# A hybrid decoder layer on one core: the queues' order from a plan in the source instead of from the framework

## The chip, the cores and the metric

One core of a Trainium2 chip runs the whole program. The metric is the device time of one execution in microseconds (us). PE is the matrix engine (PEld its weight loads), DVE the vector engine, ACT the scalar engine, POOL the general one, SP the queue that issues most of the DMAs. Each engine takes its instructions in the order in which they were issued to it, and waits on semaphores for the others.

## The reference

One layer over 1024 tokens of 1024 channels, in float32: a token mixer with two groups, then an MLP.

```python
h = rms_norm(x, g_mix_norm)
q, kc, vc, ks_, vs_, kw_, vw_, gl, hc, cg, bg = split(h @ w_in)
k_cmp, v_cmp = compress(kc), compress(vc)       # small two-layer MLPs over blocks of 32 tokens
# 8 heads of 64 in 2 groups; per head three causal softmax branches with a distance penalty:
#   compressed blocks, selected blocks of 64 tokens (16 of 16: all), a window of 512 tokens
attn_out = sum over branches of sigmoid(gl) * softmax(...) @ v
conv_out = bg * short_conv(cg * hc)             # 3 taps per channel
x = x + concat(rms_norm(attn_out), rms_norm(conv_out)) * g_out @ w_o
x = x + square(relu(rms_norm(x, g_ffn_norm) @ w_up)) @ w_down      # 1024 -> 4096 -> 1024
```

## The kernel before

Every large product is computed in float32 by three products of the PE's faster 32-bit type: each operand is split into a high part (an ACT copy, `copy_act`, line 69) and a low part (a subtraction on DVE or POOL, `tt`, line 66), and `mm3` (lines 76 to 78) issues high x high, high x low and low x high into one PSUM bank. The whole order of the source is one pass over these stages:

- Norm of x, transposed into `hTh`/`hTl` (eight blocks of 128 tokens, `tb`); the input product by tokens for keys, values, gates and queries (`zp`), with the steps of the compression (`compress_steps`, a generator) taken in between; then the convolution's channels (`zc`).
- The convolution's half of the output product (`wc`), and the keys' transposes.
- Attention, by token block in the order `ORDER` and by head group g. `scores` writes score products into two PSUM banks (`s_`, lines 509 and 510), DVE adds the penalty, copies them to `pt` and finds the extreme in one instruction (line 517, `nm`), ACT takes the exponential (line 523). `weigh` transposes the probabilities (line 618, `tp`), splits them into `ph` and `pl`, multiplies by the values (lines 630 and 631, `ot`), transposes back (`ops`, line 638) and adds to `osb`. Its steps are kept in the list `filler` and are spread by hand over the scores of the next group. `queries` loads `qx` from DRAM and transposes it (`tpq`, line 544). `finish` does the output product of one block (`wa`) and the norm's factor for the MLP.
- The MLP runs as Strassen-like products with seven instead of eight block products. `turn` (line 769) transposes differences of token blocks into the operands B11, B21, T2, T1, T3, B22, T4, through two PSUM banks (tag "up"). `up_raw` loads 1 MB of w_up for one pair of 128-wide hidden tiles and scales it by the norm's weight in eight ACT instructions. `product` splits one weight block and issues 12 matmuls; `pair` does the rest of a pair: sums into the tiles `d`, the square of the ReLU, and the stores of seven combinations to DRAM (`u_d`). The A11 and A12 products of the pairs 0 to 2 stand in the source ahead of the last transposes, as filling.
- The down product takes two pairs at a time through the same seven steps: it loads `ur`, splits it into `uu` (ten of each half, eight `ur`), splits the weights into `we` (six), and adds each PSUM result to `y`.

Buffers come from pools, which are opened and closed at the stage borders; a tile's slot is handed on in a ring. The source runs under the framework's tile scheduler with `TCARGS = dict(schedule_with_timeline_sim=True)`: the framework simulates the engines with costs of its own, and orders the queues from the order of the source. Two places override it with `tc.issue_after`: the weights of the output product are issued behind the second load of queries, and the scaling of w_up for pair q behind an ACT copy of pair q-2 (`marks`).

Of the kernel before, what the change touches and what calls it, by code (L numbers as in the profile page):

```python
# [1 line left out]

# [21 lines left out]
G = 2  # L24
# [10 lines left out]
QUADS = ((0, 1, 2, 3), (4, 5, 6, 7))  # L35
HEADS = (0, 2, 1, 3)
EPS = 1e-6
TCARGS = dict(schedule_with_timeline_sim=True)
BIG = 1e35
C_KV = AW  # L40
# [2 lines left out]
GELU_C = 0.7978845608028654  # L43


@with_exitstack
def trunk_layer(ctx, tc, x, g_mix_norm, w_in, g_q, g_k, pe_cmp, w_cmp1, b_cmp1, w_cmp2, b_cmp2,
                conv_w, g_out, w_o, g_ffn_norm, w_up, w_down, out):
    nc = tc.nc
    x2d = x.rearrange("b t d -> (b t) d")  # L50
    out2d = out.rearrange("b t d -> (b t) d")
    w_in, g_q, g_k, pe_cmp = w_in[0], g_q[0], g_k[0], pe_cmp[0]
# [3 lines left out]
    def pool(stack, name, bufs=1, side=None, space=None):  # L56
        kw = {}
        if side is not None:
            kw["side"] = side
        if space is not None:  # L60
            kw["space"] = space
        return stack.enter_context(tc.tile_pool(name=name, bufs=bufs, reuse_waits="tile", **kw))


    def tt(eng, o, a, b, op):
# [2 lines left out]
    def copy_act(o, i, scale=1.0):  # L68
        nc.scalar.activation(o, i, AF.Copy, scale=scale)  # L69
# [14 lines left out]
    cst = pool(ctx, "cst")  # L84
    st = pool(ctx, "st", bufs=3)
    ident = cst.tile([P, P], F32, name="ident")
    make_identity(nc, ident)
# [133 lines left out]
    with ExitStack() as b1:  # L221
# [129 lines left out]
        for tb, ps in (a for tbs in QUADS for a in z_tokens(pieces, tbs, 512, steps, 1)):  # L351
# [12 lines left out]
                                               dup(gq_bc), op0=ALU.mult, op1=ALU.mult)  # L364
            nc.scalar.dma_start(q_d[tb * P:(tb + 1) * P], qn.rearrange("p h a d -> p (h a d)"))


    with ExitStack() as b2:
        mcp = pool(b2, "mcp", side="right")
# [57 lines left out]
        KH = [kp.tile([P, KW], F32R, name=f"KH{g}") for g in range(G)]  # L427
        KL = kp.tile([P, KW], F32R, name="KL")
        half = [slice(g * HD, (g + 1) * HD) for g in range(G)]
        VC.append(kp.tile([P, G, P], F32R, name="vco"))  # L430
        nc.gpsimd.memset(VC[1][:64].bitcast(F32), 0.0)
        copy_act(VC[1][64:], VC[0][:64].bitcast(F32))

        def split_keys(g, c0, n, ps):
            copy_act(KH[g][:, c0:c0 + n], ps)
# [159 lines left out]
    with ExitStack() as c_:  # L595
# [3 lines left out]
        pq = pool(c2, "pq", bufs=2, side="right")  # L599
        pts.append(pool(c2, "pt1", side="right"))  # L600
        wo_pc = []

        def load_wo():
            for c in range(4):
                wo_pc.append(w_piece(wov[:, c:c + 1], [P, 1, D], gcol=G_OUT + c,
                                     alloc=lambda sh: (e1.tile(sh, F32, name="w_raw", tag="x"), wo_p.tile(sh, F32R, name="w_hi"), wo_p.tile(sh, F32R, name="w_lo"))))
# [189 lines left out]
        marks = {}  # L796

        def up_raw(q):
            raw = (ex.tile([P, KD, 2 * P], F32, name="wu", tag="x") if q % 3 == 0 else
                   vp.tile([P, KD, 2 * P], F32, name="wu", tag=("vs", "vw")[q % 3 - 1]))  # L800
            nc.sync.dma_start(raw, wuv[:, :, q * 2 * P:(q + 1) * 2 * P])
            with tc.issue_after(marks[q - 2]) if q > 2 else ExitStack():
                for k in range(KD):
                    copy_act(raw[:, k], raw[:, k], scale=cols[:, G_FFN + k:G_FFN + k + 1])
            return {f"A{i + 1}{j + 1}": raw[:, 4 * j:4 * j + 4, i * P:(i + 1) * P] for i in range(2) for j in range(2)}

        def w_unit():
# [86 lines left out]
    def pair(q, A, ps, done):  # L894
        D0, D1, D2, D3 = [None] * 4

        def square(a):
            nc.vector.scalar_tensor_tensor(a, a, 0.0, a, op0=ALU.max, op1=ALU.mult)  # L898
# [43 lines left out]
        nc.scalar.activation(D1[:, 0], D1[:, 0], AF.Square)  # L942
# [52 lines left out]
    for c in range(NPAIR // CHUNK):  # L995
        qs = range(c * CHUNK, (c + 1) * CHUNK)
        Bs = [down_raw(q) for q in qs]
        if c == 0:
            for tb in [th * 4 + j for th in TH for j in range(4)]:
                yacc[tb] = ey.tile([P, D], F32, name=f"y{tb}")  # L1000
        X = [None] * 4
        for p in range(7):
            ops = []
            for i, q in enumerate(qs):
                ur = eu.tile([P, 512], F32, name="ur", bufs=8)
                nc.sync.dma_start(ur, u_d[q][p])
                u = split([eU.tile([P, 512], F32R, name="uu", tag=f"u{h}", bufs=10) for h in "hl"], ur,
                          nc.gpsimd if i else nc.vector)
                w = split(w_unit(), down_comb(Bs[i], WANT[p]), nc.vector if i else nc.gpsimd)
                ops.append((u, w))  # L1010
            if c == 0 and p in (0, 1):
                for tb in range(TH[p] * 4, TH[p] * 4 + 4):
                    nc.sync.dma_start(yacc[tb], x2_d[tb * P:(tb + 1) * P])
            ih, n = ACC[p]
            for j in range(4):
                if p == 0:
                    X[j] = bank_p("X") if j < 3 else bank_1("X")
                elif p in (4, 6):
# [37 lines left out]
```

## Time and profile before

| | us |
|---|---|
| median of 3 runs | 1308.02 (1307.35 to 1308.24) |
| the profiled execution | 1307.12 |
| its span in the profile | 1305.3 |
| PE busy | 1251.2 |
| DVE busy | 886.9 |
| POOL busy | 685.0 |
| ACT busy | 668.8 |

The span holds 18564 instructions. A busy time counts the time in which at least one instruction of an engine runs; matmuls are pipelined, and their ends are modelled. The granted clock is the share of its full rate at which PE was allowed to run; its mean over the span is 0.984.

### The profile page before, as it was taken

The page shows a single profiled execution, that of the slowest core. Times are in us where ns is not written, and L with a number is a line of the kernel's source. Part 1 is how long each engine was busy: PE and PEld are TensorE (multiplying, and loading weights), DVE is VectorE, ACT ScalarE, POOL GpSimd, SP SyncE. Part 2 cuts the span into 40 slices and gives each one's busy share as a digit, 9 for nine tenths or more (in the row PEclk, how much of TensorE's full clock was granted, in tenths as well). Part 3 has the DMA queues.
Part 4 walks back from the last instruction along what each step waited for, and adds up shares of the span by engine and source line. Part 5 has one row for each costly group of instructions (what it writes and reads, how often), then busy time and mean ns, then how long its engine had stood idle before and what let it go on. Part 6 is the DMA issues. An engine that isn't in the chain of part 4 may idle for free.

```text
span 1305.3 us, 18564 instructions
## 1 busy us (share of the span) xinstructions
PE 1251.2 (96%) x6170; PEld 1038.4 (80%) x6170; DVE 886.9 (68%) x1869; ACT 668.8 (51%) x1498; POOL 685.0 (52%) x583
## 2 busy tenths in 40 slices
PE   6999999999999999999789999999998999999998
PEld 5898888888778778788567888888886878888887
DVE  5467863344798878988675665554557877777775
ACT  6344542111698877877834545545534434444441
POOL 2144222220133332311491897787788998988881
PEclk9999999999999999999787999999999999999999
DMA  6243531112310100000311454434548644334413
GB/s 228 71 118 107 174 116 49 49 44 77 123 40 34 49 33 34 10 17 18 113 44 65 138 182 162 161 130 161 170 143 322 237 170 168 121 128 169 166 57 129
DMA packets 91576, 147.69 MB, mean 113 GB/s; under 512 B 10900, under 2 KB 45800, under 8 KB 91480
## 3 DMA queue, kind: packets, MB, share of 16 engines
q1 hardware_dynamic: 87256, 134.51, 30.9%
q10 hardware_dynamic: 3456, 9.44, 1.9%
q0 software_dynamic: 768, 2.56, 0.7%
q8 instruction: 49, 0.80, 0.2%
q14 instruction: 47, 0.39, 0.1%
HBM read 102.43 MB, written 44.04 MB: 112 GB/s over the span
## 4 chain that ended last, share of the span: by engine, by line
PE 79%; DVE 7%; POOL 4%; ACT 4%; DMA 3%; issue 3%; SPq 0%; POOLq 0%; DVEq 0%; ACTq 0%
PE X L76 8%; PE X L77 8%; PE X L78 8%; PE Z L77 5%; PE Z L78 5%; PE Z L76 5%; PE tp L618 4%; PE zc L76 3%; PE zc L78 3%; PE zc L77 3%; PE ot L631 2%; PE ot L630 2%; PE zp L78 2%; PE zp L77 2%; PE zp L76 2%
## 5 line engine op out<-in xcount | busy, mean ns | idle before, releaser
L69 ACT ACTIVATE uu<-ur 128x512 fp32r<-128x512 f32 x112 | 69.2, 625 | 161.4 <-PE X L77 93.7
L66 POOL TENSOR_TENSOR d<-d 128x512 f32<-128x512 f32 x64 | 96.5, 1509 | 22.0 <-DVE d L898 13.0
L66 DVE TENSOR_TENSOR pl<-tp,ph 128x512 fp32r<-128x512 f32 (+1 forms) x148 | 95.0, 654 | 11.5 <-ACT ph L69 10.6
L523 ACT ACTIVATE pt<-pt,nm 128x640 f32<-128x640 f32 (+7 forms) x128 | 93.9, 736 | 14.9 <-DVE nm L517 14.7
L76 PE MATMUL X<-we,uu 128*128 128x512 f32 x256 | 97.0, 392 | 3.6 <-DVE y L66 3.6
L77 PE MATMUL X<-we,uu 128*128 128x512 f32 x256 | 100.4, 392 | 0.0
L66 DVE TENSOR_TENSOR y<-X,y 128x512 f32<-128x512 f32 x128 | 85.7, 683 | 21.4 <-PE X L78 20.6
L78 PE MATMUL X<-we,uu 128*128 128x512 f32 x256 | 99.9, 391 | 0.0
L69 ACT ACTIVATE ph<-tp 128x512 fp32r<-128x512 f32 (+1 forms) x148 | 81.9, 573 | 21.4 <-PE tp L618 20.1
L66 DVE TENSOR_TENSOR we<-s,we 128x512 fp32r<-128x512 f32 x42 | 42.8, 1018 | 69.2 <-ACT we L69 69.2
L69 ACT ACTIVATE w_hi<-w_raw,cols 128x128 fp32r<-128x128 f32 (+3 forms) x128 | 53.3, 486 | 70.6 <-PE zc L77 35.4
L66 POOL TENSOR_TENSOR uu<-ur,uu 128x512 fp32r<-128x512 f32 x56 | 88.6, 1585 | 0.0
L618 PE MATMUL tp<-ident,pt 128*128 128x128 f32 x528 | 81.9, 277 | 3.6 <-DVE pl L66 1.8
L66 DVE TENSOR_TENSOR uu<-ur,uu 128x512 fp32r<-128x512 f32 x56 | 63.6, 1139 | 30.4 <-PE X L77 15.8
L157 DVE SCALAR_TENSOR_TENSOR w_lo<-w_raw,cols,w_hi 128x128 fp32r<-128x128 f32 (+3 forms) x128 | 54.0, 468 | 36.7 <-ACT w_hi L69 36.5
L618 PEld LDWEIGHTS tp<-ident,pt 128*128 128x128 f32 x528 | 63.3, 142 | 17.0 <-DVE pl L66 2.8
L76 PE MATMUL zc<-hTh,w_hi 128*128 128x512 f32 x192 | 75.1, 391 | 1.4 <-ACT z L69 1.4
L66 DVE TENSOR_TENSOR y<-Z,y 128x512 f32<-128x512 f32 x96 | 65.0, 684 | 16.7 <-PE Z L78 16.7
L77 PE MATMUL Z<-we,uu 128*128 128x512 f32 x192 | 74.9, 390 | 1.3 <-POOL we L66 1.3
L69 ACT ACTIVATE we<-s 128x512 fp32r<-128x512 f32 x55 | 34.8, 633 | 79.8 <-PE X L77 53.9
L77 PE MATMUL zc<-hTl,w_hi 128*128 128x512 f32 x192 | 74.8, 390 | 0.0
L78 PE MATMUL zc<-hTh,w_lo 128*128 128x512 f32 x192 | 74.8, 389 | 0.0
(1289 smaller groups left out, 3968.3 us busy)
## 6 DMA issues: line engine op xcount, KB each, us to landing
u_d<-d SPq DMA_DIRECT2D x112, 256.0 KB, 2.1
ur<-u_d SPq DMA_DIRECT2D x112, 256.0 KB, 2.7
wu<-in_w_up_dram SPq DMA_DIRECT2D x16, 1024.0 KB, 5.6
wd<-in_w_down_dram SPq DMA_DIRECT2D x16, 1024.0 KB, 6.2
w_raw<-in_w_in_dram SPq DMA_DIRECT2D x20, 512.0 KB, 3.7
xt<-in_x_dram SPq DMA_DIRECT2D x10, 512.0 KB, 8.6
w_raw<-in_w_cmp_dram SPq DMA_DIRECT2D x8, 512.0 KB, 4.0
q_d<-qn ACTq DMA_DIRECT2D x8, 512.0 KB, 2.8
```

The costliest lines, as they stand in the source:

```text
L66: eng.tensor_tensor(o, a, b, op=op)
L69: nc.scalar.activation(o, i, AF.Copy, scale=scale)
L76: nc.tensor.matmul(ps, ah, bh, start=first, stop=False, **kw)
L77: nc.tensor.matmul(ps, ah, bl, start=False, stop=False, **kw)
L78: nc.tensor.matmul(ps, al, bh, start=False, stop=last, **kw)
L157: nc.vector.scalar_tensor_tensor(lo[:, j], raw[:, j], c, hi[:, j].bitcast(F32), op0=ALU.mult, op1=ALU.subtract)
L523: nc.scalar.activation(dst[b], dst[b], AF.Exp, bias=nm[:, b, sl:sl + 1], scale=-1.0, accum_out=sm[:, b, sl:sl + 1])
L618: nc.tensor.transpose(tp[:, i], a, ident)
L630: nc.tensor.matmul(o, v, ph, start=first, stop=False)
L631: nc.tensor.matmul(o, v, pl, start=False, stop=last)
```

## The change

All of the source's calls go to a recorder. `Plan` stands in for the engines and the pools: each call becomes a node (up to four matmuls into the same tile make one), and reading and writing regions of tiles, opening and closing pools and taking slots become edges. At the end `issue` makes a list schedule: five queues, a cost for each instruction as a formula of its form and size, one line for all DMAs, and priority by the longest remaining path, in which the reuse of a ring's slots counts as an edge. Tiles take their slots in recorded order, and a pool opens when all users of the pools closed before it have ended in the plan. Then the real calls are made in the planned order, under `manual_schedule` for all five engines, so that the framework only sets the semaphores.

```diff
+ENGINES = {mybir.EngineType.PE, mybir.EngineType.Activation, mybir.EngineType.DVE, mybir.EngineType.Pool,
+           mybir.EngineType.SP}
...
+    def cost(self, name, method, a, kw, views):          # returns occupancy, time to the result, bytes
+        n = max([v.cols() for _, v in views], default=1)
+        psum = any(v.base.pool.psum for k, v in views if k not in ("out", "accum_out"))
+        if method == "dma_start":
...
+            return (.75 if name == "POOL" else .33), 0.0, nb
+        if name == "PE":
+            if method == "transpose":
+                c = .109
+            else:
...
+                c = max(4 * c / 4560, .218) if rhs.base.args[1] == F32 else max((c if c >= 256 else 4 * c) / 2400 + .014, .109)
+            return c, c + .17, 0
+        if name == "ACT":
+            c = .06 + n * .00093 if n >= 600 else max(.085 + n * .00079 if n > 100 else .17 + n * .0008, .17)
+            acc = kw.get("accum_out") is not None
+            return c + .1 * acc, c + (.1 if acc else .11), 0
+        if name == "DVE":
...
+            if method == "tensor_tensor":
+                c = (.06 + n * .00106) * (1.45 if not psum and n >= 256 else 1.0)
...
+            return max(c, .08), c + .08, 0
+        if method == "tensor_tensor":                     # POOL
...
+            c = .18 + n * .00215
+            return c, c + .03, 0
...
+    def schedule(self, weight=lambda n: 0.0, rings=True):
...
+        for n in reversed(topo):
+            own = .4 + n.bytes / .36e6 + 1.75 if n.bytes else n.late
+            n.prio = own + max([s.prio for s in n.succ + more[n.k]], default=0.0)
...
+            best = None
+            for e in names:
+                if ready[e]:
+                    t = free[e]
+                elif wait[e]:
+                    t = max(free[e], wait[e][0][0])
...
+                if best is None or t < best[0]:
+                    best = t, e
...
+            while wait[e] and wait[e][0][0] <= t + 1e-9:
+                k = heapq.heappop(wait[e])[1]
+                heapq.heappush(ready[e], (-nodes[k].prio, k))
+            n = nodes[heapq.heappop(ready[e])[1]]
+            n.start = t
+            free[e] = t + n.busy
+            done = t + n.late
+            if n.bytes:
+                line = max(t + .4, line) + n.bytes / .36e6
+                done = line + 1.75
...
+    def issue(self):
+        end, order = self.schedule()
...
+        with self.tc.manual_schedule(engines=ENGINES):
+            for n in order:
+                for f in n.do:
+                    f()
...
-    nc = tc.nc
+    plan = Plan(tc)
+    nc = plan.nc
...
+        for _ in steps:
+            pass
...
-        VC.append(kp.tile([P, G, P], F32R, name="vco"))
-        nc.gpsimd.memset(VC[1][:64].bitcast(F32), 0.0)
-        copy_act(VC[1][64:], VC[0][:64].bitcast(F32))
...
+        VC.append(pq.tile([P, G, P], F32R, name="vco", bufs=1))
+        nc.gpsimd.memset(VC[1][:64].bitcast(F32), 0.0)
+        copy_act(VC[1][64:], VC[0][:64].bitcast(F32))
...
-                    with tc.issue_after(q_load[1].ins):
-                        load_wo()
+                    load_wo()
...
-            with tc.issue_after(marks[q - 2]) if q > 2 else ExitStack():
-                for k in range(KD):
-                    copy_act(raw[:, k], raw[:, k], scale=cols[:, G_FFN + k:G_FFN + k + 1])
+            for k in range(KD):
+                copy_act(raw[:, k], raw[:, k], scale=cols[:, G_FFN + k:G_FFN + k + 1])
...
-        marks[q] = nc.scalar.activation(D1[:, 1], ps["Z"], AF.Copy).ins
+        copy_act(D1[:, 1], ps["Z"])
...
+    plan.issue()
```

Besides, the identity matrix is built by the two POOL instructions in the source that the framework's helper issued, the steps of the compression that were left over for the convolution's loop are recorded ahead of it, and the tile `vco` (a copy of the compressed values on the other half of the partitions) is built in a pool of the attention stage.

More of the change, by code (lines that the diff above doesn't have):

```diff
@@ L43, with axes, side @@
 GELU_C = 0.7978845608028654
+SPACE = np.ndarray((1 << 24,), np.int8)
+BASE = SPACE.__array_interface__["data"][0]
+def axes(pattern, shape, sizes):
+    def side(s):
+        out, group = [], None
+        for w in s.replace("(", " ( ").replace(")", " ) ").split():
+            if w == "(":
+                group = []
+            elif w == ")":
+                out.append(group)
+                group = None
+            elif group is None:
+                out.append([w])
+            else:
+                group.append(w)
+        return out
+    left, right = (side(s) for s in pattern.split("->"))
+    sizes = dict(sizes)
+    for names, n in zip(left, shape):
+        known = 1
+        for w in names:
+            known *= sizes.get(w, 1)
+        for w in names:
+            sizes.setdefault(w, n // known)
+    flat = [w for names in left for w in names]
+    return [sizes[w] for w in flat], [flat.index(w) for names in right for w in names], \
+        [int(np.prod([sizes[w] for w in names])) for names in right]
@@ new lines, with __init__, step, __getitem__ @@
+class View:
+    def __init__(self, base, shadow, ops):
+        self.base, self.shadow, self.ops = base, shadow, ops
+    def step(self, shadow, op):
+        return View(self.base, shadow, self.ops + (op,))
+    def __getitem__(self, k):
+        return self.step(self.shadow[k], lambda a: a[k])
+    def rearrange(self, pattern, **sizes):
+        split, order, merged = axes(pattern, self.shadow.shape, sizes)
+        s = self.shadow.reshape(split).transpose(order).view()
+        s.shape = merged
+        return self.step(s, lambda a: a.rearrange(pattern, **sizes))
+    def bitcast(self, dt):
+        return self.step(self.shadow, lambda a: a.bitcast(dt))
+    def unsqueeze(self, k):
+        return self.step(np.expand_dims(self.shadow, k), lambda a: a.unsqueeze(k))
+    def to_broadcast(self, shape):
+        return self.step(np.broadcast_to(self.shadow, shape), lambda a: a.to_broadcast(shape))
+    def real(self):
+        a = self.base.tile
+        for op in self.ops:
+            a = op(a)
+        return a
+    def cols(self):
+        return int(np.prod(self.shadow.shape[1:]))
+    def region(self):
+        s = self.shadow
+        off = s.__array_interface__["data"][0] - BASE
+        key = (off, s.shape, s.strides, self.base.row)
+        if key not in REGIONS:
+            pos = np.zeros((1,), np.int64) + off
+            for n, st in zip(s.shape, s.strides):
+                if st:
+                    pos = np.unique((pos[:, None] + np.arange(n) * st).ravel())
+            row, col = pos // self.base.row, pos % self.base.row // 4
+            bits = np.zeros(self.base.row // 4, np.uint8)
+            bits[col] = 1
+            REGIONS[key] = int(row.min()), int(row.max()) + 1, int.from_bytes(np.packbits(bits).tobytes(), "big")
+        return REGIONS[key]
@@ new lines, with __init__ @@
+REGIONS = {}
+class Node:
+    def __init__(self, k, engine):
+        self.k, self.engine, self.do, self.preds, self.succ = k, engine, [], set(), []
+        self.busy = self.late = self.bytes = 0.0
+        self.base, self.bases = None, []
+class Base:
+    def __init__(self, pool, shape, dtype, kw):
+        self.pool, self.args, self.kw = pool, (shape, dtype), kw
+        n = int(np.prod(shape))
+        self.row = n // shape[0] * 4
+        self.shadow = SPACE[:n * 4].view(np.int32).reshape(shape)
+        self.seen, self.nodes, self.tile = [], [], None
@@ L61, in pool @@
             kw["space"] = space
-        return stack.enter_context(tc.tile_pool(name=name, bufs=bufs, reuse_waits="tile", **kw))
+        return stack.enter_context(plan.pool(name=name, bufs=bufs, reuse_waits="tile", **kw))
     def tt(eng, o, a, b, op):
@@ L86, in trunk_layer @@
     ident = cst.tile([P, P], F32, name="ident")
-    make_identity(nc, ident)
+    nc.gpsimd.memset(ident, 0.0)
+    nc.gpsimd.affine_select(out=ident, in_=ident, pattern=[[-1, P]], compare_op=ALU.not_equal, fill=1.0, base=0,
+                            channel_multiplier=1)
     mhalf = cst.tile([P, H], F32, name="mhalf")
```

216 lines of the change are left out of this document (214 added, 2 removed).

## The prediction

> **What bounds the kernel now.** I read the page's engine totals first, then its 40 slices, then cut the span at the places where the slices dip and asked for the busy time of each engine in those stretches.
>
> ```profile
> PE 1251.2 (96%) x6170; PEld 1038.4 (80%) x6170; DVE 886.9 (68%) x1869; ACT 668.8 (51%) x1498; POOL 685.0 (52%) x583
> PE   6999999999999999999789999999998999999998
> PEclk9999999999999999999787999999999999999999
> ...
> 0.00:24.00 24.00, 13.03 (x55) 10.18 (x55) 11.04 (x25) 16.66 (x30) 7.29 (x25) 1.00 0.81 275
> 24.00:320.00 296.00, 293.50 (x1482) 249.41 (x1483) 168.34 (x417) 105.00 (x255) 77.32 (x86) 1.00 0.31 92
> 320.00:341.00 21.00, 19.30 (x91) 15.61 (x90) 10.13 (x32) 7.29 (x20) 1.96 (x4) 0.99 0.24 88
> 341.00:621.00 280.00, 268.81 (x1648) 224.61 (x1646) 242.99 (x822) 230.61 (x603) 75.53 (x114) 0.99 0.10 35
> 621.00:704.00 83.00, 65.56 (x306) 50.98 (x305) 52.92 (x74) 44.12 (x88) 43.94 (x37) 0.79 0.21 67
> 704.00:980.00 276.00, 275.50 (x1215) 227.68 (x1213) 153.06 (x162) 140.53 (x280) 216.25 (x146) 1.00 0.46 155
> 980.00:1056.00 76.00, 70.24 (x300) 57.18 (x300) 61.22 (x74) 31.92 (x58) 68.04 (x45) 0.98 0.69 248
> 1056.00:1280.00 224.00, 224.00 (x990) 185.47 (x988) 173.22 (x247) 90.31 (x165) 192.07 (x128) 1.00 0.41 138
> 1280.00:1305.30 25.30, 21.24 (x94) 17.27 (x92) 13.97 (x19) 2.31 (x4) 2.59 (x2) 1.00 0.45 167
> ```
>
> The columns are the stretch, its length, then PE, PEld, DVE, ACT and POOL busy with their counts, the granted clock, the DMA share and GB/s. PE is the bound: it is busy for 1251.2 of 1305.3 us. A new order can give back only its 54.1 us of idle time and what the low clock cost. The two long stages of the MLP (704 to 980 and 1056 to 1280) have 0.5 us of PE idle time in 500. Three places hold most of the rest: the start (11.0), the attention (341 to 621: 280 - 268.8 = 11.2), and above all the passage from attention to the MLP (621 to 704): 83 - 65.6 = 17.4 us idle, and a mean clock of 0.79 over 65.6 busy us, which is 65.6 x 0.21 = 13.8 us more. So 31 us lie in those 83.
>
> Why PE stands still there is told by the timeline and by windows of 4 us:
>
> ```profile
> 635.07 3.30 ACT L69 ACTIVATE wu<-wu,cols 128x256 f32<-128x256 f32 x8 [0.94 <-DMA wu<-in_w_up_dram]
> 639.63 1.11 PE L769 MATMUL tp<-ident,y 128*128 128x128 f32 x4 [4.78 <-DVE B11l L66]
> 639.71 3.30 ACT L69 ACTIVATE wu<-wu,cols 128x256 f32<-128x256 f32 x8
> 643.41 3.30 ACT L69 ACTIVATE wu<-wu,cols 128x256 f32<-128x256 f32 x8
> 678.44 1.08 PE L769 MATMUL tp<-ident,y 128*128 128x128 f32 x4 [2.94 <-DVE T2l L66]
> ...
> 636.00:640.00 4.00, 0.37 (x2) 0.38 (x3) 1.12 (x2) 4.00 (x10) 1.24 (x2) 0.69 1.05 373
> 644.00:648.00 4.00, 1.54 (x6) 1.14 (x6) 1.67 (x4) 4.00 (x11) 1.32 (x2) 0.50 0.00 0
> 652.00:656.00 4.00, 4.00 (x22) 3.28 (x21) 3.71 (x4) 0.96 (x2) 4.00 (x4) 1.00 0.01 2
> 680.00:684.00 4.00, 1.75 (x7) 1.35 (x8) 3.84 (x5) 1.71 (x3) 3.23 (x3) 0.50 0.40 100
> ```
>
> ACT scales three pieces of w_up (three rows of eight, 9.9 us) in one run, ahead of the small copies for which PE waits; PE stands 4.78 us, its clock falls to 0.50, and it is back at 1.00 only in 652 to 656. At 678 it happens again: the transposes of the last tokens (line 769) wait for a DVE subtraction queued behind weight splits, and the products that could have filled the time have been spent by then.
>
> **The change part by part.** The same instructions with the same tiles are issued; PE's work isn't altered. What is new is the order on each queue, worked out ahead from costs written in the source. Priority is the longest remaining path, and the paths run through the reuse of buffers too.
>
> *Passage, 621 to 704.* In the old order ACT takes the 24 scalings as they come. By path length the copies behind the last attention tile come first, since the whole last x row hangs on them (output product, norm, differences, five transposes, then every later pair), while the scalings of pairs 1 and 2 have slack; and the six products ready early stay available as filling. The floor of the stage is the greater of PE's work at full clock, 65.6 x 0.79 = 51.8 us, and DVE's 52.9 us, so at most 83 - 53 = 30 us can go. The low bound: only the first gap closes, 4.8 us and about as much of clock, say 9. I take 20, two thirds of the ceiling, because the transposes still share two PSUM banks in recorded order, and DVE would have to be full from end to end to reach 30.
>
> The clock follows from those gaps: 4.78 us idle took it to 0.50, while in the attention, whose longest PE wait is 1.3 us (below), it stays at 0.99. [...]
>
> *Attention, 341 to 621.*
>
> ```profile
> PE tpq L544 <- DMA qx<-q_d: 2.6, 4, 1.3
> PE s__3522 L509 <- DVE nm L517: 0.9, 1, 0.9
> PE s__4203 L509 <- DVE nm L517: 0.5, 1, 0.5
> L517 DVE DVE_READ_ACCUMULATOR2_ANT nm<- 128x1 f32 x257 | 21.1, 82 | 0.0
> L66 DVE TENSOR_TENSOR pl<-tp,ph 128x512 fp32r<-128x512 f32 (+1 forms) x135 | 86.5, 652 | 9.7 <-ACT ph L69 8.9
> L69 ACT ACTIVATE ph<-tp 128x512 fp32r<-128x512 f32 (+1 forms) x136 | 75.2, 572 | 17.2 <-PE tp L618 15.9 <-PE ot L630 0.7
> ```
>
> Three engines run close together here: PE 269, DVE 243, ACT 231 of 280 us. The qx loads (2.6 us of PE waiting) can be issued ahead; the short waits behind nm can be filled by either branch. At best 8 of the 11.2 go. Against that, PE is now told to take a score matmul at the moment the plan thinks its bank is free. The plan's cost for these two evacuations is good: 0.60 us of occupancy and 0.68 to the result for the DVE one against 0.652, and 0.49 and 0.60 for the ACT one against 0.572. I take +3, and leave the loss to the first rival.
>
> *The MLP stages, 704 to 980 and 1056 to 1280.* Nothing can be won; what can be lost is what mis-sized costs expose.
>
> ```profile
> L66 DVE TENSOR_TENSOR we<-wu,we 128x512 fp32r<-128x512 f32 x38 | 51.3, 1357 | 13.6 <-ACT we L69 13.6
> L66 POOL TENSOR_TENSOR d<-d 128x512 f32<-128x512 f32 x64 | 96.5, 1509 | 22.0 <-DVE d L898 13.0 <-ACT d L942 7.9
> L66 POOL TENSOR_TENSOR uu<-ur,uu 128x512 fp32r<-128x512 f32 x56 | 88.6, 1585 | 0.0
> 1088.00:1120.00 32.00, 32.00 (x143) 26.50 (x142) 24.34 (x36) 13.19 (x24) 27.11 (x19) 1.00 0.48 165
> ```
>
> The plan has 0.87 us for a DVE operation on two SBUF operands, and the trace 1.36 while POOL works too; 1.28 for POOL, and 1.51 to 1.59. So the plan is early by up to 0.5 us on operands of products. What covers it is depth: six weight units and eight u tiles. A matmul starts every 32/143 = 0.224 us, a step of the down stage has 24 of them, 5.4 us, and uses two u tiles, so the loads may run four steps, 21 us, ahead. The new fixed SP queue, where a store of u that waits for POOL holds up the loads behind it, is covered the same way; without the cover each would cost its 0.2 to 0.5 us. I take -3 for both stages, between 0 and -5. The scalings, once tied behind a copy of two pairs before (marks), are now held by priority alone: nothing, as PE is the bound there.
>
> *The rest.*
>
> ```profile
> 8.68 1.57 PEld L195 LDWEIGHTS tp<-ident,xt 128*128 128x128 f32 x8 [1.18 <-DVE xt L190]
> 340.31 0.96 PE L544 MATMUL tpq<-ident,qx 128*128 128x128 f32 x4 [1.13 <-DMA qx<-q_d]
> 998.49 0.50 PE L76 MATMUL X<-we,uu 128*128 128x512 f32 x1 [3.63 <-DVE y L66]
> ```
>
> Start: the first x rows reach PE at 8.7 us by load, norm and scaling, and no order shortens that chain; of the other 2.3 us idle I take +1. From 24 to 341 there are 2.5 + 1.7 us idle, of which the qx load is 1.1: +2. At 980 to 1056 (5.8 us idle, 3.63 in one wait), the first down products still need the up stage's pools closed, then a load and a split: +1 of 5.8. The tail waits for the last sums and stores in either order: 0. The vco tile is built in another pool and the end of the compression is recorded earlier: a handful of small operations, hidden while PE has 293.5 busy us of 296; uncovered, a few tenths.
>
> Sum: 1 + 2 + 3 + 20 - 3 + 1 = 24 us. The profiled execution took 1307.1 us (span 1305.3 and 1.8 around it), 0.9 under the median of 1308.0. 1307.1 - 24 = 1283. With the bounds, the forecast's own range is 1307.1 - 46 = 1261 (30 + 8 + 2.3 + 4.2 + 1.5, no loss) to 1307.1 - 9 + 5 = 1303.
>
> **The rivals.**
>
> *First rival, slower: the attention's hand-offs are exposed.* Place: 341 to 621, where DVE is 87% busy and two score banks are handed between PE and DVE; line 517 ends 257 such reductions. PE takes what the plan says even if the other branch is ready; the old order has the same weakness, but with waits on only a few of them. One exposed hand-off costs about 0.5 us (rows of nm: 0.9 and 0.5). The other terms are worth 21 us, so it decides from 42 of 257, one in six; with one in three it is 86 x 0.5 = 43 us: 1307.1 - 21 + 43 = 1329. For it: DVE has little slack, and a fixed order can't answer a late engine. Against: the costs there agree with the trace within a tenth. Chance 0.20.
>
> *Second, slower: many short waits lower the clock.* In 621 to 704 PE was 79% busy and had a clock of 0.79. If half of the attention came to that, 134 busy us at 0.79 would take 36 more: 1307.1 - 21 + 36 = 1322. Against: with PE 96% busy in short pieces the clock is 0.99 now. Chance 0.06. [...]
>
> *Third, slower: the stage gates.* In the plan a pool opens only once all that used the closed pools has ended. Three such closings lie between the last scores and the first pair; if they put the first w_up work later, two new gaps of 5 us with as much of clock come while the old ones stay: +20, 1327. For it: the same closings stand in both. Against: the order is fixed by them, but the real waits are per tile. Chance 0.08.
>
> *Fourth, no change.* Buffers are handed out in recorded order in both, so the same order may come out: 1305 to 1310. Chance 0.04.
>
> **How the numbers follow.** Forecast 0.62 at 1283; the rest as above. All but 0.04 lie beyond 0.2% (2.6 us), about what a measurement of this kernel can tell. Faster 0.62, same 0.04, slower 0.34. The range starts at the forecast's best, 1260, and reaches into the first three rivals, to 1326; I leave out about half of their chance, as their prices lie around 1322 to 1329, and a few hundredths below.
>
> **What would show it.** Right: in the passage, the 24 scalings are spread out, no PE wait there is above 2 us, its clock is above 0.9, and it is some 20 us shorter; the attention has about its 280 us, and the MLP stages stay at full PE. Wrong: PE waits for nm, ph or pl in dozens in the attention (first rival), a clock below 0.95 with no long gap (second), or new gaps of some us at the stage borders (third).

## The result, and the profile after

The changed kernel took 1322.6 us (median of 4 runs, 1318.9 to 1328.0) against 1308.1 (4 runs, 1307.4 to 1308.2): a ratio of 1.0115, 95% interval 1.0075 to 1.0155. It is 14.5 us slower, where 24 less were forecast; the time lies inside the range, on the wrong side. The profiled execution is the fastest of the four, 1318.9 us with a span of 1317.1, so 3.7 us of the median lie outside what the profile shows.

From the page of the changed kernel, engine totals and PE's slices:

```profile
PE 1248.7 (95%) x6170; PEld 1031.2 (78%) x6170; DVE 909.9 (69%) x1869; ACT 674.1 (51%) x1498; POOL 672.9 (51%) x583
PE   6999899999889999999899999999999899999998
PEclk9999899999999999999899999999999999999999
```

The same 6170 matmuls; the mean clock rose from 0.984 to 0.991, and the idle time from 54.1 to 1317.1 - 1248.7 = 68.4 us. All calls are now issued from one line (261), so the readings go by tiles.

Where the time went is told by three matmuls that mark stage borders: the last of the convolution's output product (wc), the first on T2 (the last operand of the passage that is needed for the first pair), and the first of the down product (X<-we,uu). The rows of the tile view give the first and the last start of a group; before, then after:

```profile
L78 PE MATMUL wc<-w_hi,MCl x64: 388/389/476, 286.2 to 335.8; 128*128 128x512 f32 x64
L76 PE MATMUL X<-T2h,we x64: 388/389/775, 695.6 to 979.1; 128*128 128x512 f32 x64
L76 PE MATMUL X<-we,uu x256: 387/389/629, 989.3 to 1286.1; 128*128 128x512 f32 x128
```

```profile
L261 PE MATMUL wc<-w_hi,MCl x64: 387/389/478, 292.5 to 343.0; 128*128 128x512 f32 x64
L261 PE MATMUL X<-T2h,we x128: 389/389/501, 678.9 to 967.6; 128*128 128x512 f32 x128
L261 PE MATMUL X<-we,uu x768: 387/389/792, 986.5 to 1306.5; 128*128 128x512 f32 x192
```

With the span they cut each execution into four stages (us). The table holds the experiments too, cut in the same way from their own rows:

| kernel | start to last wc | attention and passage | up | down | span | median |
|---|---|---|---|---|---|---|
| before | 335.8 | 359.8 | 293.7 | 316.0 | 1305.3 | 1308.1 |
| after | 343.0 | 335.9 | 307.6 | 330.6 | 1317.1 | 1322.6 |
| e1_marks | 346.3 | 334.7 | 295.5 | 333.5 | 1310.0 | 1313.9 |
| e2_dma | 337.5 | 342.3 | 295.6 | 328.9 | 1304.3 | 1304.4 |
| e3_pow | 338.2 | 333.3 | 308.4 | 333.9 | 1313.8 | 1319.5 |
| e4_group | 339.9 | 345.7 | 305.0 | 318.3 | 1308.9 | 1314.4 |
| e5_marksgroup | 340.3 | 344.2 | 293.4 | 318.9 | 1296.8 | 1299.8 |
| e6_comb | 333.4 | 348.7 | 294.0 | 320.0 | 1296.1 | 1297.2 |
| e7_order | 353.5 | 359.0 | 320.4 | 324.0 | 1356.9 | 1358.9 |
| e8_costs | 332.7 | 340.1 | 298.2 | 326.1 | 1297.1 | 1299.5 |
| e9_mlpnodes | 344.7 | 340.1 | 291.8 | 318.9 | 1295.5 | 1297.7 |
| e10_pow_mlpnodes | 338.6 | 338.2 | 291.7 | 318.0 | 1286.5 | 1288.7 |
| e11_costs_mlpnodes | 333.1 | 342.3 | 292.3 | 321.2 | 1288.9 | 1289.8 |

From before to after: +7.2, -23.9, +13.9, +14.6, together the 11.8 us between the two spans. So the gain that was forecast is there, and three losses, for which the forecast had next to nothing, outweigh it.

The borders are not quite clean, because work moves across them. Ahead of the last wc product stand 32 score products and 8 transposes of queries before, and 18 and 4 after; they took 4.9 us of PE's time before and 2.3 after. Ahead of the first T2 product stand 73 products of the up stage before and 57 after (0.227 us each from start to start), and 8 more transposes after (0.109 each). Counted for equal work, an estimate from these prices, the four differences are about +9.9, -23.8, +11.1 and +14.6.

The start of the last score product cuts the second stage in two, the attention and the passage. The rows of the passage, before and after, with the columns of the prediction's stretches:

```profile
618.10:695.60 77.50, 60.16 (x297) 47.04 (x296) 52.09 (x76) 43.73 (x89) 43.28 (x36) 0.80 0.22 72
624.60:678.90 54.30, 48.69 (x281) 39.41 (x279) 48.14 (x73) 41.48 (x85) 42.63 (x37) 0.94 0.28 93
```

The passage is 23.2 us shorter, or 20.4 for equal work, and its clock is 0.94 where it was 0.80. The attention took 282.3 us before and 281.6 after, with 2.7 us more work in it.

The gain, from windows of 4 us and ACT's timeline of the changed kernel:

```profile
640.00:644.00 4.00, 2.22 (x15) 1.48 (x14) 3.76 (x6) 4.00 (x10) 3.12 (x4) 1.00 0.47 166
644.00:648.00 4.00, 1.77 (x9) 1.77 (x10) 3.92 (x5) 3.55 (x9) 3.70 (x4) 0.57 0.02 4
652.00:656.00 4.00, 4.00 (x26) 3.33 (x25) 4.00 (x6) 4.00 (x11) 3.49 (x4) 1.00 0.01 2
...
649.15 0.90 ACT L261 ACTIVATE wu<-wu,cols 128x256 f32<-128x256 f32 x2
650.08 0.63 ACT L261 ACTIVATE we<-wu 128x512 fp32r<-128x512 f32 x1
651.22 0.60 ACT L261 ACTIVATE T1h<-tp 128x512 fp32r<-128x512 f32 x1 [0.51 <-PE tp L261]
651.71 1.30 ACT L261 ACTIVATE wu<-wu,cols 128x256 f32<-128x256 f32 x3
```

The scalings come in pieces of one to four between the copies for which PE waits. One dip of the clock is left, at 644 to 652, and the second one, at 676 to 700 before, is gone.

### The profile page after: what moved, and what is told of

It reads as the page before. It is cut to its first block, busy times and chain, and to the rows that moved or that the text cites. A ratio compares the mean times of both kernels' runs of the same rounds, so it can differ in the third digit from the quotient of the medians.

```text
span 1317.1 us, 18392 instructions
## 1 busy us (share of the span) xinstructions
PE 1248.7 (95%) x6170; PEld 1031.2 (78%) x6170; DVE 909.9 (69%) x1869; ACT 674.1 (51%) x1498; POOL 672.9 (51%) x583
## 5 line engine op out<-in xcount | busy, mean ns | idle before, releaser
L261 PE MATMUL X<-we,uu 128*128 128x512 f32 x768 | 186.4, 393 | 13.3 <-DVE y L261 7.3
L261 PEld LDWEIGHTS X<-we,uu 128*128 128x128 f32 x768 | 144.0, 189 | 49.1 <-issue 7.0
L261 PE MATMUL Z<-we,uu 128*128 128x512 f32 x576 | 139.0, 392 | 2.7 <-DVE y L261 2.7
L261 PEld LDWEIGHTS Z<-we,uu 128*128 128x128 f32 x576 | 109.1, 190 | 25.9 <-ACT uu L261 3.1
L261 ACT ACTIVATE we<-wd 128x512 fp32r<-128x512 f32 x64 | 40.5, 632 | 124.6 <-PE X L261 83.6
L261 POOL TENSOR_TENSOR uu<-ur,uu 128x512 fp32r<-128x512 f32 x56 | 80.0, 1432 | 32.7 <-ACT uu L261 32.7
L261 ACT ACTIVATE ph<-tp 128x512 fp32r<-128x512 f32 (+1 forms) x148 | 82.5, 573 | 20.1 <-PE tp L261 18.2
L261 PE MATMUL tp<-ident,pt 128*128 128x128 f32 x528 | 88.7, 275 | 3.4 <-ACT pt L261 1.7
L261 ACT ACTIVATE wu<-wu,cols 128x256 f32<-128x256 f32 x128 | 55.8, 509 | 37.2 <-DMA wu<-in_w_up_dram 37.2
L261 DVE TENSOR_TENSOR we<-wu,we 128x512 fp32r<-128x512 f32 x38 | 50.5, 1341 | 34.1 <-ACT we L261 34.1
L261 POOL TENSOR_TENSOR osb<-osb,ot_s 128x256 f32<-128x256 f32 x64 | 48.4, 756 | 45.2 <-DVE ot_s L261 39.1
```

Of the source, the lines that this page charges most:

```text
L261: node.do.append(lambda: getattr(engine, method)(*[real(x) for x in a], **{k: real(x) for k, x in kw.items()}))
```

## The experiments

All are the changed kernel with one or a few edits to its planner. The kernel before was run beside them each time (medians 1308.7 to 1309.3, against 1308.1 beside the changed kernel); the changed kernel was not run again. How much a stage varies without any change of order is seen in the start: the changed kernel, e1_marks and e9_mlpnodes issue the same sequence there on PE, DVE, ACT and POOL, and it took 343.0, 346.3 and 344.7 us.

### e1_marks and e2_dma: the up stage

Where PE lost its time there is told by its waits in 704 to 960 of the changed kernel (total, times, longest), and by ACT's timeline at one of them:

```profile
PE Z L261 <- ACT d L261: 4.8, 6, 1.3
PE X L261 <- ACT d L261: 2.7, 5, 1.1
...
794.11 0.58 ACT L261 ACTIVATE d<-X 128x512 f32<-128x512 f32 x1
799.12 0.91 ACT L261 ACTIVATE wu<-wu,cols 128x256 f32<-128x256 f32 x2 [4.44 <-DMA wu<-in_w_up_dram]
799.94 0.61 ACT L261 ACTIVATE we<-s 128x512 fp32r<-128x512 f32 x1
800.46 0.57 ACT L261 ACTIVATE d<-Z 128x512 f32<-128x512 f32 x1
...
801.08 0.50 PE L261 MATMUL Z<-B22h,we 128*128 128x512 f32 x1 [0.98 <-ACT d L261]
```

The plan had put a scaling of the next pair ahead of the copy of bank Z. The load had not landed, ACT stood 4.44 us at the head of its queue, Z was copied at 800.5, and PE's next product into Z came late. e1 puts back, as edges of the plan, the order that the old kernel had by hand:

```diff
+        marks = {}
...
             for k in range(KD):
                 copy_act(raw[:, k], raw[:, k], scale=cols[:, G_FFN + k:G_FFN + k + 1])
+                if q > 2:
+                    plan.nodes[-1].preds.add(marks[q - 2].k)
...
         copy_act(D1[:, 1], ps["Z"])
+        marks[q] = plan.nodes[-1]
```

> The plan with one edge per scaling put back: the scaling of w_up for pair q may only be planned behind the ACT copy of PSUM of pair q-2, as the kernel before had it. Theory A (the plan puts the scalings at the moment it thinks the 1 MB load has landed; ACT then waits for the load at the head of its queue, and the copies of PSUM behind it are late): the 37.2 us in which ACT waits for loads of w_up fall below 8, matmuls per 32 us in 704 to 960 rise from 135 or 136 to 140 or more, and the time falls by 8 to 14 us. Rival B (PE takes the products in turns of four matmuls, so that several sums end together and their evacuations come at once): ACT's waits go, but the time falls by less than 3 us.

1313.9 us, 8.7 below the kernel after the change; the up stage went from 307.6 to 295.5, with the same products in it. ACT no longer waits for a load of w_up anywhere in 700 to 960, and PE's list of waits for 704 to 960 is empty.

e2 raises the plan's fixed time of a DMA:

```diff
-            own = .4 + n.bytes / .36e6 + 1.75 if n.bytes else n.late
+            own = .4 + n.bytes / .36e6 + 3.75 if n.bytes else n.late
...
-                done = line + 1.75
+                done = line + 3.75
```

> Only the plan's fixed time of a DMA is raised, from 1.75 to 3.75 us, so a load of 1 MB is planned at 7.1 us instead of 5.1 (it took 6.0 in the profile after the change). Theory A: ACT's waits for loads of w_up fall from 37.2 us to below 10, the up stage gains 8 to 14 us, and the repeated runs spread less than the 9 us they had. Rival B: less than 3 us. If the later planning of all other loads opens gaps at the start or at the stage borders, some of it is lost again there.

1304.4 us, 18.2 below the kernel after the change, and a little below the kernel before (ratio 0.9960, interval 0.9943 to 0.9976). The up stage took 295.6. A load of 1 MB is planned at 7.1 us now, which is above the 6.0 that it took, so this is a margin rather than a correction. The expectation on ACT's waits missed; these are one stretch of the up stage in the changed kernel, in e1 and in e2, with e2's wait:

```profile
740.00:950.00 210.00, 203.81 (x886) 165.29 (x885) 112.86 (x117) 101.10 (x206) 158.50 (x106) 1.00 0.43 145
```

```profile
740.00:950.00 210.00, 209.91 (x927) 173.48 (x926) 125.87 (x122) 107.34 (x219) 169.81 (x111) 1.00 0.48 158
```

```profile
740.00:950.00 210.00, 209.89 (x926) 173.19 (x925) 136.96 (x121) 107.61 (x214) 166.83 (x112) 1.00 0.47 154
ACT wu L261 <- DMA wu<-in_w_up_dram: 36.7, 12, 4.7
```

e1 and e2 are full, with 927 and 926 matmuls in 210 us where the changed kernel has 886. In e2 ACT waits for loads as long as ever (36.7 us against 37.2), and it does no harm, because nothing that PE needs stands behind it:

```profile
773.06 0.58 ACT L261 ACTIVATE d<-Z 128x512 f32<-128x512 f32 x1
...
778.77 2.11 ACT L261 ACTIVATE wu<-wu,cols 128x256 f32<-128x256 f32 x5 [4.62 <-DMA wu<-in_w_up_dram]
```

Z is copied 5.7 us ahead of the scaling that waits. So it isn't the waiting that costs, as theory A was put, but which copy of PSUM is queued behind the wait. The changed kernel has twelve such waits in 704 to 960. Seven stand between a copy of X and the copy of Z, and behind six of these PE stops for Z, for the 4.8 us of the row above; behind the five that follow a copy of Z it doesn't stop. In e2 eleven of the twelve follow a copy of Z. e2 also shortened the start by 5.5 us and lengthened the middle by 6.4: every load moved in the plan.

### e3_pow: the start

The one long stop of PE in the start, and ACT's and DVE's rows around it:

```profile
127.24 0.60 ACT L261 ACTIVATE z<-zp 128x512 f32<-128x512 f32 x1 [5.47 <-DVE qn L261]
129.51 1.64 POOL L261 TENSOR_TENSOR qri<-rs_t,mhalf 128x8 f32<-128x8 f32 x1 [5.09 <-DVE rs_t L261]
131.18 0.17 DVE L261 TENSOR_TENSOR qri<-qri,qscale 128x8 f32<-128x8 f32 x1 [1.75 <-POOL qri L261]
135.57 0.41 DVE L261 COPY hT<-tp 128x256 f32<-128x256 f32 x1
136.08 1.09 PE L261 MATMUL cps<-w,hT 128*128 128x64 f32 x4 [7.60 <-issue]
```

The plan has 0.5 us for the power of eight columns; it takes 1.64. DVE waits in order for the result (1.75 us here, 7.9 in six of the eight), ACT waits for DVE (its copy of z is behind the store of q), and the small product cps, planned between two others, holds PE for 7.6 us. The profile names nothing that cps waited for ("issue"), but its operand hT was copied by DVE just ahead of it, and that copy stands in DVE's order behind the products of the queries' norm that wait for the power. Nearly the whole loss of the start lies here: in 120 to 180 PE was busy for 49.9 us, and for 58.6 before.

```diff
-                return .5, .56, 0
+                return (.5, .56, 0) if n == 1 else (.42 + .17 * n, .48 + .17 * n, 0)
```

> Only the plan's cost of POOL's power instruction is changed: 0.5 us for one column as before, 0.42 + 0.17 per column for more (1.78 for eight, as the profile has it, instead of 0.5). Theory C (the plan thinks the norm of the queries is 1.3 us shorter for each token block than it is, the copies of PSUM fall behind, and PE runs dry at 128 to 136): the gap of 7.6 us and the lower clock after it go, 8 to 12 us less. Rival (the gap comes from the in-order ACT queue, where the store of q waits for DVE whatever the plan thinks): less than 3 us.

1319.5 us: 3.1 less in the medians, whose runs overlap, and the start 4.8 us shorter in the profiles. In the window 126 to 142 PE was busy 8.40 of 16 us at a clock of 0.79 after the change, and 15.80 at 1.00 in e3. A wait of 3.7 us came up later, for the compression's hidden layer. So the cost explains about half of what was expected; the same loss was removed by other edits too (e2), which speaks for a plan that is tight there rather than for one wrong number.

### e4_group and e5_marksgroup: the down stage

DVE's timeline across the border of two pairs, in the changed kernel:

```profile
1081.01 2.48 DVE L261 TENSOR_TENSOR y<-X,y 128x512 f32<-128x512 f32 x4
1083.40 0.81 DVE L261 TENSOR_TENSOR we<-T,we 128x512 fp32r<-128x512 f32 x1
1084.13 1.77 DVE L261 TENSOR_TENSOR uu<-ur,uu 128x512 fp32r<-128x512 f32 x1
1085.82 1.78 DVE L261 TENSOR_TENSOR we<-T,we 128x512 fp32r<-128x512 f32 x1
1087.53 2.47 DVE L261 TENSOR_TENSOR y<-X,y 128x512 f32<-128x512 f32 x4
```

The sums into y come four at once. A step has four banks, each with six matmuls; the plan's nodes hold four, so PE takes four for each bank in turn, then the last two of each, and all four banks are done together. PE's timeline shows it with two steps in turn, 16 of one and 16 of the other, then the last eight of each:

```profile
1059.82 3.79 PE L261 MATMUL X<-we,uu 128*128 128x512 f32 x16
1063.45 3.79 PE L261 MATMUL Z<-we,uu 128*128 128x512 f32 x16
1067.07 1.98 PE L261 MATMUL X<-we,uu 128*128 128x512 f32 x8
1068.89 1.98 PE L261 MATMUL Z<-we,uu 128*128 128x512 f32 x8
```

The sums then stand behind splits of 1.8 us, and the next step's first matmul waits for them (0.81 us in that wait). e4 lets a node hold more:

```diff
-    GROUP = 4
+    GROUP = 12
```

> Only the size of a PE node is changed: up to 12 matmuls into the same tile are one node instead of 4, so a product of the MLP is taken in one piece. Rival B (turns of four matmuls let sums end together): the up stage loses its waits for copies of PSUM, the down stage its wait of 0.8 us per two pairs, together 15 to 25 us less. Theory A: the ACT waits for loads stay near 37 us and the up stage gains less than 4 us; the down stage, where no load is in the way, may gain up to 12.

1314.4 us, 8.2 less. The sums are spread, and the down stage is full; e4's timeline, then the stretch 1090 to 1250 before, after and in e4:

```profile
1085.29 1.42 DVE L261 TENSOR_TENSOR y<-X,y 128x512 f32<-128x512 f32 x2
1087.37 0.69 DVE L261 TENSOR_TENSOR y<-X,y 128x512 f32<-128x512 f32 x1 [0.67 <-PE X L261]
1088.04 1.54 DVE L261 TENSOR_TENSOR we<-wd,we 128x512 fp32r<-128x512 f32 x1
1089.50 0.68 DVE L261 TENSOR_TENSOR y<-X,y 128x512 f32<-128x512 f32 x1
```

```profile
1090.00:1250.00 160.00, 160.00 (x707) 132.50 (x707) 123.88 (x177) 64.39 (x118) 139.76 (x94) 1.00 0.44 148
```

```profile
1090.00:1250.00 160.00, 156.32 (x682) 127.05 (x682) 130.14 (x170) 64.64 (x112) 127.86 (x91) 1.00 0.45 145
```

```profile
1090.00:1250.00 160.00, 160.00 (x708) 132.52 (x707) 142.86 (x178) 66.75 (x117) 139.21 (x94) 1.00 0.45 148
```

707 matmuls in 160 us before, 682 after, 708 in e4. The up stage took 305.0, and with nodes of twelve 73 of its products stand ahead of its border instead of 57, 3.6 us of work; so the turns of four are no part of its loss. ACT's waits for loads there, expected near 37 us, rose to 68.4. The middle (attention and passage) grew by 9.8 us, which was not expected; some 3 of them are the work that moved. e5 has both edits:

> Both cures of the MLP stages in one: the scalings' edge of e1 and the nodes of up to 12 matmuls of e4. e1 made the up stage full (260 us of PE in 260) and left the down stage as it was; e4 made the down stage full (224 of 224) and left the up stage. Theory A+B (two separate causes, one in each stage): the gains add, 8.7 + 8.2 us below the kernel after the change, so 1304 to 1308, and both stages are full. Rival (with one cause gone the other's waits come back elsewhere): above 1311.

1299.8 us, 22.7 below the kernel after the change, more than the sum of 8.7 and 8.2 and better than the 1304 to 1308 expected; up 293.4, down 318.9, both full (928 matmuls in 740 to 950, 707 in 1090 to 1250). Each edit mends its own stage, so the two causes are separate.

### e6_comb, e8_costs, e7_order: costs and priority

> All four edits: DMA time 3.75, the power's cost by columns, nodes of up to 12 matmuls, the scalings' edge. If the four losses are separate and the passage's gain of some 20 us stays, the time is 1290 to 1300, below the kernel before. Rival (each new set of costs shifts the whole plan by chance, and the single results don't add): 1303 to 1315.

1297.2 us, as the first theory had it, though only 2.6 below e5: the start is 6.9 us better, the middle 4.5 worse.

e8 corrects costs alone: those of e2 and e3, and

```diff
-                c = (.06 + n * .00106) * (1.45 if not psum and n >= 256 else 1.0)
+                c = (.06 + n * .00106) * (2.1 if not psum and n >= 256 else 1.0)
-            c = .18 + n * .00215
+            c = .18 + n * .0026
```

> Only costs are corrected, all three: DMA 1.75 to 3.75 us, the power by columns, and for operations on two SBUF operands DVE's factor 1.45 to 2.1 (0.87 to 1.26 us for 512 columns) and POOL's slope (1.28 to 1.51 us), as the profiles have them. e2 alone gave 1304.4. If mis-sized costs are behind most of the loss, also of the down stage where y's sums wait behind weight splits: 1295 to 1302 and a down stage with 140 or more matmuls in 32 us. Rival B (the down stage's loss is the turns of four): the down stage stays at 137, and the time at 1300 to 1306.

1299.5 us, 23.1 below the kernel after the change, with no edge added and the small nodes kept. The down stage gained 4.5 us against the 12.3 of e4, and reached 139 matmuls in 32 us, between the 137 and the 140 that were to tell the theories apart: there the turns of four are the greater part, and the costs the smaller. With the DMA's time alone e2 had 18.2 of the 23.1 us.

e7 changes the priority:

```diff
-            n.prio += weight(n)
+            n.prio = -n.k
```

> The plan as changed, with its costs, pools and nodes, but the priority is the order of recording instead of the longest remaining path. Theory P (the priority by path length made the gain in the passage from attention to the MLP): the 24 scalings and the old order come back there, the passage is some 15 to 20 us longer, and the turns of four matmuls in the MLP go, since a product's nodes are recorded one after another; the time is near the kernel before, 1305 to 1320. Rival (the costs and the list made the gain, whatever the priority): the passage stays short, and the time falls below 1305.

1358.9 us, 36.3 above the kernel after the change, more than either theory had. The middle is back at 359.0 (before: 359.8), but only in part for the reason of theory P. Cut as above, the attention took 292.8 us instead of 281.6, and this is e7's passage:

```profile
646.30:712.50 66.20, 55.05 (x310) 43.25 (x309) 52.69 (x79) 46.67 (x99) 43.10 (x37) 0.93 0.27 88
```

It is 11.9 us longer than after the change (8.7 for equal work) and 11.3 shorter than before, and the scalings come in pieces of eight, three, five, five, one and two, not all 24 in one run. So the priority by path length made somewhat less than half of the passage's gain; what in the plan made the rest was not tested. Recorded order did not cure the up stage, which came to 320.4: PE waited 18.9 us in ten places for ACT's copies of Z, at most 3.2.

### e9 to e11: the best version

The large nodes for the MLP's tiles only:

```diff
-        if (last is not None and last.out is out.base and len(last.do) < self.GROUP and method == "matmul" and
+        if (last is not None and last.out is out.base and len(last.do) < (12 if out.base.kw["name"] in ("X", "Z", "W") else self.GROUP) and method == "matmul" and
```

> As e5 (scalings' edge and nodes of up to 12 matmuls), but the large nodes only for the MLP's products (PSUM tiles X, Z, W); all others keep four. In e4 and e5 the stretch from the last wc product to the first T2 product took 344 to 346 us instead of 336. Theory D (the large nodes hold up the critical chain in the attention, where a transposed block needs PE at once): that stretch goes back to 334 to 337 us, the MLP stages stay at 293 to 295 and 318 to 320, and the time is 1288 to 1293. Rival (that stretch is long because of what the products of the MLP do in the passage): it stays at 344, the time at 1298 to 1301.

1297.7 us. The middle came back to 340.1, and as in e4 16 more products of the up stage stand in it, 3.6 us; without them it is 336.5, so theory D holds for this stretch. The time missed its range because the start was the long one again (344.7, with the stop of 7.7 us at cps).

> As e9, with the power's cost by columns too. In e3 this alone took the start up to the last wc product from 343.0 to 338.2 us. If the parts add: 3 to 5 us below e9, 1284 to 1290. Rival (start and MLP are not independent): the same as e9.

1288.7 us: 9.0 below e9, where 3 to 5 were expected. The start gave 6.1 of them (344.7 to 338.6).

> All the cost corrections of e8, the scalings' edge and the large nodes in the MLP only. From the stages' best: start 333 (e8), middle 334 to 340, up 294, down 318 to 320, with 1.8 around it: 1281 to 1288. Rival (the longer DMA time in the plan lengthens the middle, as in e2 with 342 and e8 with 340): 1288 to 1294.

1289.8 us: the start is 5.5 us better than in e10, the middle 4.1 and the down stage 3.2 worse. The rival holds. e10 has the lowest median, though the runs of the two overlap: the scalings' edge, the power's cost, and large nodes in the MLP. It beats both kernels, with a ratio of 0.9841 to the kernel before (interval 0.9826 to 0.9856), and its four runs lie within 1.2 us. Its page and one stretch of each MLP stage:

```profile
PE 1240.7 (96%) x6170; PEld 1032.0 (80%) x6170; DVE 931.9 (72%) x1869; ACT 676.2 (53%) x1498; POOL 684.2 (53%) x583
740.00:950.00 210.00, 210.00 (x928) 173.90 (x927) 125.68 (x123) 108.45 (x214) 164.35 (x113) 1.00 0.47 152
1090.00:1240.00 150.00, 150.00 (x664) 124.20 (x663) 133.66 (x167) 63.76 (x111) 129.30 (x87) 1.00 0.45 141
```

## Why the prediction was wrong

*The passage and the attention were right.* +20 and +3 were forecast and 23.9 came, for equal work 20.4 in the passage and 3.4 in the attention. The scalings are spread, one clock dip is gone, and the passage's mean clock is 0.94. That the sizes fit so closely is partly luck, since 20 was taken as two thirds of a ceiling. Of the reason that was given, the priority by path length, e7 bears out somewhat less than half. One sign missed: the passage still holds a PE wait of 2.7 us.

*The failing step is "The MLP stages": -3, between 0 and -5.* It measured -28.5 (13.9 and 14.6), or -25.7 for equal work. The cover that it named, the depth of six weight units and eight u tiles, is cover for operands, and operands weren't late. What was late was the way out: copies and sums that free a PSUM bank. There the cover is thin: in the source all X products of a pair share one bank, and the four banks of a down step are used again by the next; ACT and DVE take the copies and sums in order. Two single sentences went wrong:

- "The scalings, once tied behind a copy ... are now held by priority alone: nothing, as PE is the bound there." This edge was worth 12.1 us of the up stage (e1). The working asked what the scalings wait for, and not what is queued behind them on ACT. The wait of 4.44 us at the head of the queue is of the kind that was priced for SP's loads and was not looked for on ACT.
- The nodes of four matmuls stood in the change's description and had no term at all. They cost 12.3 us in the down stage (e4).

*The start*, +1 and +2 forecast up to 341, lost 7.2 us (9.9 for equal work). The row of the power of eight columns was on hand in the trace of before and was not held against the plan's 0.5 us; e3 gives 4.8 for it, and e10 against e9 6.1. The rest of this term is open: e2, which leaves the power alone, gains 5.5.

*The mis-sized costs* were seen (1.36 against 0.87 us, and 1.51 against 1.28), and were put down as harmless. Two DVE splits of 1.77 and 1.78 us ahead of the sums show the effect. The trace after the change has 0.68 to 1.78 us for the same split of uu. The 31 splits of uu and we on DVE beside an idle POOL took 0.68 to 0.69 us, and the 81 with POOL at work for over 95% of their time took 1.41 on average (0.68 to 1.83), while y's sums, which read one operand from PSUM, stay at 0.67 to 0.69 beside a working POOL too. What in POOL's work decides between 0.68 and 1.83 us was not shown. With all three costs raised the plan came out at 1299.5 (e8), on the forecast's side; most of that came with the DMA's time, which was set above the 6.0 us of the profile.

*The rivals.* The first had the kind of failure right (hand-offs exposed in a fixed order) and the place wrong. In the attention PE hardly waits for DVE's reductions; these are the largest waits there after the change (total, times, longest):

```profile
PE wa L261 <- DVE ml L261: 2.6, 2, 1.7
PE tp L261 <- ACT pt L261: 1.7, 4, 0.6
PE s__3307 L261 <- DVE nm L261: 1.0, 1, 1.0
```

The second rival, short waits that lower the clock, decided nothing here: the attention's clock is 0.99 in both kernels, and 704 to 960 lost 5% of its matmuls to short waits at a clock of 1.00. But waits of at most 1.13 us came before a fall to 0.50 at 340.5 in the kernel before (last section). Of the third, new gaps at the stage borders, a part is seen: at 986.5 and 989.8 the down product starts with waits of 2.16 and 2.58 us for its splits, where there was one of 3.63. Two more, of 2.74 and 3.18 us at 1027 and 1049, are waits for y's sums, and no such wait is left there in e4.

## What to carry to other kernels

A queue in a fixed order must be read from the waiting instruction backwards: ask what stands behind it, above all the copies that free a PSUM bank, and put an instruction that depends on a load behind them and not ahead (12.1 us of the up stage here). When a list schedule cuts long accumulations into pieces, it can take them in turns, as here: all sums end together, and the evacuation comes in a clump. Keep an accumulation in one piece where PE is full (12.3 us of the down stage here). A plan that is made once is only as good as its costs: raising three of them was worth 23 us here, about what the passage and the attention had gained. And when stages are compared across two orders, count the work between the borders first, since products move across them.

## What was not expected of the hardware, and what is open

- The runs of the changed kernel spread over 9.2 us (1318.9 to 1328.0), and those of e10 over 1.2. With the same order on every queue in every run, something outside it decides. The granted clock goes with it: 0.991, 0.990, 0.987 and 0.982 for 1318.9, 1320.1, 1325.0 and 1328.0 us, and 0.009 of some 1249 busy us is 11 us. Why the clock fell more in some runs was not settled: the loads' landing at the head of ACT's queue would fit, but e2, whose ACT waits as long, spreads over 4.0.
- The same edit gave different gains in different company: the power's cost 3.1 us alone and 9.0 in e10, e1 and e4 together more than their sum. A part of this is the spread of the changed kernel, from which all of them are counted. The plan is one chain of choices, and a new cost anywhere moves loads and slots elsewhere. Why the large nodes lengthen the middle in e4 by more than the work that moved, some 6 us, half in the attention and half in the passage, was not followed further.
- No single long wait is needed for PE's clock to fall. The traces before and after the change hold nine falls from 1.00 to 0.50 (leaving out the last 8 us of each), and the stretches at 0.50 that follow them last 3.4 us or a multiple of it, up to 20.5. In the 3.4 us before each fall PE was busy for at most 50% of the time, by the profile's modelled times, and its longest unbroken idle time in them was between 1.1 and 3.4 us. The changed kernel, for example, has a fall at 388.6: PE was busy for 1.64 us from 385.2 to 388.6, with 1.71 us as the longest wait, and the clock was 0.50 until 392.0. The kernel before has one at 340.5, after waits of at most 1.13 us. So the prediction's account, which sets a wait of 4.78 us against waits of 1.3 us, is too simple: what these nine falls have in common is how little PE did in the 3.4 us before. It is no full rule, since two such stretches of the changed kernel with as little work (45% busy from 159.9 to 163.3, 48% from 1044.0 to 1047.4) passed without a fall.
